# A decode step on one Trainium2 core: set-up reordered around the first tile, norm factors in two parts, a denser cache stream

## The chip, the core and the metric

One core of a Trainium2 chip runs the whole program. The metric is the device time of one execution in microseconds (us). TensorE (PE in the profile) does the matmuls and transposes, VectorE (DVE), ScalarE (ACT) and GpSimd (POOL) the elementwise work; SP issues the plain DMAs and GpSimd the gathers. All arithmetic is fp32: a matmul operand is split into a high and a low part (names ending in hi and lo, or wh and wl), and three products replace one.

## What is computed

One layer step for 512 prompt tokens and 32 sample tokens (8 sequences of 4), whose attention reads a paged cache of 4096 past positions each.

```python
q, k, v, u, gv = split_proj(rms_norm(hp, norm_mix[l]), w_in[l],
                            q_gain[l], k_gain[l], gv_gain[l])
att = prompt_diff_attn(q, k, v, lam)
mix = chunk_gating(u, gv, w_spatial[l], b_spatial[l], GMLP_CHUNK)
hp = hp + merge_out(att, mix, subln_gain[l], lam_init, w_out[l])
hp = hp + sq_relu_ffn(hp, norm_ffn[l], w_up[l], w_down[l])
...
k_past = cache_k[l][page_table].reshape(n_seq_d, n_pages * PAGE_SIZE, N_ATT_HEADS, 2, QK_DIM)
v_past = cache_v[l][page_table].reshape(n_seq_d, n_pages * PAGE_SIZE, N_ATT_HEADS, V_DIM)
att_s = sample_diff_attn(qs, kns, vns, k_past, v_past, lam)
```

`rms_norm` divides by the root mean square and multiplies by a gain; q, k and gv are normalised again per head. `sample_diff_attn` is a softmax over past and new positions, twice per head, and the difference of the two. The model width is 1024, the feed-forward width 4096.

## The kernel before

**Main work.** After `setup`, `in_proj` runs ten pieces of W_in, 256 columns each, in the order q, q, k, k, v, v, gv, gv, u, u. A piece has two halves of the weights' rows and four token tiles of 128; `optB` does a tile and half in 12 matmuls of 128x256 (the block of 12 that the text speaks of). `packed` does the sample tokens' share of a piece in 16 matmuls, from `spk`, the packed sample input. `w_conv` splits a weight half: ScalarE casts wh, VectorE subtracts to get wl. `x_tile` transposes a prompt tile and `split` makes its Thi (ScalarE) and Tlo (VectorE). `post` and `finish_piece` make the norm factors: squares are summed in `ssb`, `rsqrt` raises them to -1/2 on GpSimd (a POOL instruction with `mhalf`), VectorE multiplies (`zn<-zn,ssb`), TensorE transposes (`d<-idt,zn`). Then come the prompt's attention, W_out and eight groups of the feed-forward (`ffn`).

**The stream.** The sample tokens' attention over the cache runs beside this, in 64 chunks of 1 MB of keys and 1 MB of values. `gK` and `gV` gather them (two buffers `kraw`, four `v`), `k_tr` transposes keys on VectorE (kt<-kraw), and issues the gather of chunk n+2 into the buffer it frees; `scores` does two chunks in one block of matmuls (S, the score block, 32 records in the trace), `av` multiplies by values (O), and `fin1`, `fin2` close a sequence: VectorE copies O into `om`, TensorE sums it by a selection matrix (om,selb). `qz_fill` writes a sequence's queries into `qz`. These steps are a list, `micro`; the main work yields a cost after each stretch, and `pump` issues as many steps as the cost pays for, at `TAU` per unit of weight.

**The order.** Each engine runs its instructions in program order. `pinned(True)` keeps the written order; otherwise a scheduler may move instructions of TensorE and VectorE forward, past up to 28 others. Before, `setup` issues the sample input, the page table, the gain in 128 copies (`gm`, 512 KB), weights 0 and 1, prompt tile 0, weights 2 and 3 and the other tiles, and multiplies prompt tiles by `gm` ahead of their transposes (`x_gain`). The sample's queries of both q pieces come ahead of the first piece (`first_q`, `first_keys`), `k_tr` of chunks 0 and 1 with them, and the stream starts there. The third weight half has a buffer of its own, `wq`.

Of the kernel before, what the change touches and what calls it, by code (L numbers as in the profile page):

```python
# [62 lines left out]
def kernel(  # L63
# [88 lines left out]
    wq = big.tile([128, 4 * T], F32R, tag="r3", name="wq")[:, 0:2048].rearrange("p (s k c) -> p s k c", s=2, k=4)  # L152
# [4 lines left out]
    xg = [R[0][:, 1024 * t:1024 * t + 1024] for t in range(2)]  # L157
# [107 lines left out]
    def w_conv():  # L265

        i = st["done"]
        if raws:
            raw = raws.pop(0)
            if i == 3:  # L270
                hi, lo = wq[:, 0], wq[:, 1]
            else:
                pool = pools["w"] if i % 5 > 2 else wp
                hi = pool.tile([128, 4, 256], F32R, tag="wh", name="wh")
                lo = pool.tile([128, 4, 256], F32R, tag="wl", name="wl")
# [119 lines left out]
    def setup():  # L395
        kt0 = kvp.tile([128, 4096], F32, tag="kt", name="kt0")
        xs = kt0[0:32, 0:1024]
        gm = kvp.tile([128, 1024], F32, tag="pp", name="gm")
        fg = kvp.tile([128, 2048], F32, tag="v", name="fg", bufs=VB)
        junk = kvp.tile([128, 512], F32, tag="om", name="junk")  # L400
        ptb = zt_().bitcast(I32).rearrange("p (n q) -> p n q", q=4)
# [11 lines left out]
        for t in range(1, 4):  # L413
            SP.dma_start(out=xt[t], in_=xp[:, t, :])

        G.memset(mhalf, -0.5)
        for t in ssb + [cst]:
            G.memset(t, 1.0)
        kw = dict(base=0, channel_multiplier=0, allow_small_or_imprecise_dtypes=True)
        G.iota(pf[:, 7:8], pattern=[[0, 1]], base=0, channel_multiplier=1, allow_small_or_imprecise_dtypes=True)  # L420
        make_identity(nc, idt)
# [7 lines left out]
        G.memset(gsrc[0:32, :], 0.0)  # L429
# [16 lines left out]
        ps = dt_()  # L446
        for k in range(8):
            PE.transpose(ps[:, 32 * k:32 * k + 32], xsg[:, 128 * k:128 * k + 128], idt[:32, :32])
        keep_warm(5)
        pack(ps[:, 0:256].rearrange("p (k t) -> p k t", k=8), 0, 8)  # L450
        w_conv()
# [4 lines left out]
        x_gain(gm, 0)  # L456
        for n in range(KB):
            gK(n)
        w_conv()
        SP.dma_start(out=gsrc[0:8, :], in_=norm_mix.rearrange("a (k p) -> (a k) p", p=128))  # L460
        SP.dma_start(out=gsrc[8:16, :], in_=norm_ffn.rearrange("a (k p) -> (a k) p", p=128))
        SP.dma_start(out=gsrc[16:20, :], in_=b_spatial.rearrange("a g t -> (a g) t"))
        SP.dma_start(out=gsrc[20:21, 0:64], in_=q_gain)
        SP.dma_start(out=gsrc[20:21, 64:128], in_=q_gain)
        SP.dma_start(out=gsrc[21:22, :], in_=subln_gain)
# [9 lines left out]
        return gm, F, gsrc, junk  # L475
# [16 lines left out]
    def gcols(gsrc):  # L492
        ps = dt_()
        PE.transpose(ps[:, 0:32], gsrc[0:32, 0:128], idt[:32, :32])
        V.tensor_copy(out=gcol, in_=ps[:, 0:32])
# [10 lines left out]
    def params():  # L506
        pinned(True)
# [16 lines left out]
        pinned(False)  # L524
# [58 lines left out]
    def scores(m):  # L583
        b, pj = divmod(m, 4)
        if pj == 0:
            qz_fill(b)
# [113 lines left out]
    TAU = (122.7 + 44.8 * G1 + 30.0 * ATTW) / sum(w for w, _ in micro)  # L700
# [14 lines left out]
    def x_gain(gm, t):  # L715
        (G if t == 3 else V).tensor_tensor(out=xg[t % 2], in0=xt[t], in1=gm, op=ALU.mult)

    def x_tile(t):
        for hf in range(2):
            ps = dt_()  # L720
            for k in range(4):
                kk = 4 * hf + k
                PE.transpose(ps[:, 128 * k:128 * k + 128], xg[t % 2][:, 128 * kk:128 * kk + 128], idt)
            split(ps.rearrange("p (k t) -> p k t", k=4), 4 * hf, t)
# [36 lines left out]
    def finish_piece(kind, p, ss, items):  # L761
# [3 lines left out]
        def stat():  # L765
            rsqrt(ss[:, 0:w * len(items)], EPS if kind in "qk" else 4.0 * EPS)
# [21 lines left out]
        later(stat)  # L788
        for i in range(len(items)):
            later(lambda i=i: norm(i), 1 + i // 2)  # L790
# [45 lines left out]
    def in_proj(gm, F, gsrc, junk):  # L836
        held = []
        pinned(True)
        zq = []

        def first_q(p):
            held.append((w_get(), w_get()))
            sps = dt_()[0:64, 0:256]
            for hf in range(2):
                packed(*held[p][hf], [(4 * hf + b, b) for b in range(4)], sps, hf == 0, hf == 1)
            return sps

        def first_stat(p, sps):
            z = combine(sps)
            zq.append(head_stat(z[0:32], 32, cst[0:32, 4 * p:4 * p + 4], 4))  # L850

        def first_keys():
            x_tile(2)
            k_tr(0)
            for p in range(2):
                q_sample(p, zq[p], cst[0:32, 4 * p:4 * p + 4])
            k_tr(1)
            kv["on"] = True

        sps = first_q(0)  # L860
        x_tile(0)
        w_conv()
        x_gain(gm, 1)
        x_stat(0, [xt[0]], 128, junk, G)
        x_gain(gm, 2)
        x_tile(1)
        x_gain(gm, 3)
        first_stat(0, sps)
        first_stat(1, first_q(1))
        rsqrt(cst[:32, 0:8], EPS)  # L870
        first_keys()
        yield 1.7
        att = attention()
        nt = new_tokens()
        for pi in range(10):
# [10 lines left out]
            if kind == "q":  # L886
                A_, B_ = held[p]
            else:
                A_, B_ = w_get(), w_get()
            for tp in range(2):  # L890
# [5 lines left out]
                for half, w in ((0, A_), (1, B_)):  # L896
                    for t in (2 * tp, 2 * tp + 1):
                        cost = next(att, 0.0) if 2 * pi + tp >= ATT0 else 0.0
                        if half == 0:
                            pss[t] = dt_()[:, 0:256]  # L900
                        optB(pss[t], t, *w, half)
                        if t == 3 and (half == 0 or pi != 1):
# [547 lines left out]
```

## Time and profile before

| | |
|---|---|
| runs | 822.18, 821.0, 822.18 us; median 822.18 |
| profiled execution | 821.3 us, its span 819.6 us |
| mean granted TensorE clock | 0.991 of full speed |
| TensorE busy | 795.7 us (97%) |
| VectorE, ScalarE, GpSimd busy | 537.1 (66%), 358.6 (44%), 178.2 us (22%) |
| DMA | 219 MB, 267 GB/s mean; gathers 134 MB of it |

The span is the time between the first and the last instruction recorded; the execution's own time is 1.7 us more. Busy shares are of the span. All helpers record their operations under line 52 (L52), so operations are told apart by the names of their tiles: `out<-in`.

### The profile page before, as it was taken

The page shows a single profiled execution, that of the slowest core. Times are in us where ns is not written, and L with a number is a line of the kernel's source. Part 1 is how long each engine was busy: PE and PEld are TensorE (multiplying, and loading weights), DVE is VectorE, ACT ScalarE, POOL GpSimd, SP SyncE. Part 2 cuts the span into 40 slices and gives each one's busy share as a digit, 9 for nine tenths or more (in the row PEclk, how much of TensorE's full clock was granted, in tenths as well). Part 3 has the DMA queues.
Part 4 walks back from the last instruction along what each step waited for, and adds up shares of the span by engine and source line. Part 5 has one row for each costly group of instructions (what it writes and reads, how often), then busy time and mean ns, then how long its engine had stood idle before and what let it go on. Part 6 is the DMA issues. An engine that isn't in the chain of part 4 may idle for free.

```text
span 819.6 us, 15373 instructions
## 1 busy us (share of the span) xinstructions
PE 795.7 (97%) x6210; PEld 632.9 (77%) x6210; DVE 537.1 (66%) x883; ACT 358.6 (44%) x892; POOL 178.2 (22%) x196
## 2 busy tenths in 40 slices
PE   5899999999999999999999999998999999999997
PEld 4888887767667888867776777675676999998997
DVE  5878866898997856887677667653464534444254
ACT  4644743776585466463144235234243431331331
POOL 4553431344241222221322321213010000000000
PEclk9799999999999999999999999999999999999999
DMA  8597698787787888877997888877459677576202
GB/s 296 207 391 280 240 344 314 272 317 285 279 321 273 309 310 309 325 283 282 366 366 304 318 325 336 322 264 261 168 182 339 209 244 239 174 239 214 70 18 94
DMA packets 101798, 219.05 MB, mean 267 GB/s; under 512 B 6090, under 2 KB 83999, under 8 KB 85343
## 3 DMA queue, kind: packets, MB, share of 16 engines
q0 software_dynamic: 18432, 134.23, 42.4%
q1 hardware_dynamic: 83294, 83.84, 31.5%
q8 instruction: 49, 0.80, 0.4%
q14 instruction: 23, 0.18, 0.1%
HBM read 213.53 MB, written 4.52 MB: 266 GB/s over the span
## 4 chain that ended last, share of the span: by engine, by line
PE 73%; DVE 8%; issue 8%; ACT 4%; DMA 3%; POOL 2%; SPq 0%; DVEq 0%; POOLq 0%; ACTq 0%
PE d L52 64%; PE S L52 5%; PE O L52 5%; DVE kt L52 2%; ACT PT L52 2%; DMA kraw<-in_cache_k_dram,idxK 2%; DMA v<-in_cache_v_dram,idxK 1%; DMA raw<-in_w_in_dram 1%; ACT wh L52 1%; POOL v L52 1%; DVE zn L52 1%; DVE s L52 1%; POOL ssb L52 1%; DVE wl L52 1%; POOL kraw L52 1%
## 5 line engine op out<-in xcount | busy, mean ns | idle before, releaser
L52 ACT CAST wh<-raw 128x1024 fp32r<-128x1024 f32 x90 | 94.2, 1047 | 175.8 <-PE d L52 139.2
L52 PE MATMUL d<-a,wh 128*128 128x272 f32 (+1 forms) x704 | 168.3, 341 | 0.0
L52 DVE STREAM_TRANSPOSE kt<-kraw 128x2048 f32<-128x2048 f32 x64 | 146.3, 2297 | 16.6 <-PE S L52 7.4
L52 DVE TENSOR_TENSOR wl<-raw,wh 128x1024 fp32r<-128x1024 f32 x90 | 109.7, 1220 | 50.8 <-ACT wh L52 50.4
L52 PEld LDWEIGHTS d<-a,wh 128*128 128x128 f32 x704 | 113.2, 188 | 25.1 <-issue 6.3
L52 PE MATMUL d<-wh,Thi 128*128 128x256 f32 x432 | 127.7, 296 | 1.6 <-ACT t L52 1.6
L52 POOL DMA_INDIRECT v<-in_cache_v_dram,idxK x64 | 64.6, 1009 | 281.3 <-PE O L52 270.9
L52 PE MATMUL d<-wl,Thi 128*128 128x256 f32 x432 | 122.9, 285 | 0.0
L52 PE MATMUL d<-wh,Tlo 128*128 128x256 f32 x432 | 122.3, 284 | 0.0
L52 PE MATMUL d<-Thi,wh 128*128 128x272 f32 (+2 forms) x368 | 108.1, 334 | 0.0
L52 PE MATMUL d<-Tlo,wh 128*128 128x272 f32 (+2 forms) x368 | 106.5, 330 | 0.0
L52 PE MATMUL d<-Thi,wl 128*128 128x272 f32 (+2 forms) x368 | 106.4, 329 | 0.0
L52 PE MATMUL d<-a,wl 128*128 128x272 f32 (+1 forms) x352 | 104.2, 337 | 0.0
L52 PEld LDWEIGHTS d<-wh,Thi 128*128 128x128 f32 x432 | 82.3, 191 | 9.0 <-issue 4.8
L52 POOL DMA_INDIRECT kraw<-in_cache_k_dram,idxK x64 | 69.6, 1088 | 83.8 <-DVE kt L52 49.9
L52 PEld LDWEIGHTS d<-wh,Tlo 128*128 128x128 f32 x432 | 82.3, 191 | 0.4 <-issue 0.4
L52 PEld LDWEIGHTS d<-wl,Thi 128*128 128x128 f32 x432 | 82.1, 190 | 0.4 <-issue 0.4
L52 PEld LDWEIGHTS d<-Thi,wh 128*128 128x128 f32 x368 | 63.5, 188 | 15.6 <-issue 5.4
L52 ACT COPY PT<-d 32x128 f32<-32x128 f32 x256 | 65.6, 256 | 10.7 <-DVE d L52 7.5
L52 PEld LDWEIGHTS d<-Thi,wl 128*128 128x128 f32 x368 | 63.4, 188 | 6.2
L52 PEld LDWEIGHTS d<-Tlo,wh 128*128 128x128 f32 x368 | 63.7, 188 | 5.8
L52 PEld LDWEIGHTS d<-a,wl 128*128 128x128 f32 x352 | 60.5, 188 | 7.4 <-issue 0.4
(270 smaller groups left out, 1063.5 us busy)
## 6 DMA issues: line engine op xcount, KB each, us to landing
raw<-in_w_up_dram SPq DMA_DIRECT2D x32, 512.0 KB, 5.5
raw<-in_w_down_dram SPq DMA_DIRECT2D x32, 512.0 KB, 5.1
plain<-in_w_up_dram SPq DMA_DIRECT2D x20, 512.0 KB, 4.9
plain<-in_w_down_dram SPq DMA_DIRECT2D x20, 512.0 KB, 5.6
raw<-in_w_in_dram SPq DMA_DIRECT2D x18, 512.0 KB, 10.1
raw<-in_w_out_dram SPq DMA_DIRECT2D x8, 512.0 KB, 10.1
plain<-in_w_out_dram SPq DMA_DIRECT2D x8, 512.0 KB, 4.6
r<-in_x_prompt_dram SPq DMA_DIRECT2D x4, 512.0 KB, 9.0
```

The source lines that it names most:

```text
L52: r = f(*args, **kw)
```

## The change

1. `setup`: prompt tile 0, the gain as 8 rows of 128 (`grow`) and weights 0 and 1 are issued first, then the sample input, tile 1, the page table, tiles 2 and 3, weights 2 and 3 (into `w23`, and `wq` goes). `gm` goes: the gain is transposed to a column (`gcol`) and applied to the transposes' result, by ScalarE's scale for tile 0 and a VectorE product for the others (`x_half`).
2. `in_proj`: the first piece goes tile by tile, each tile made one step ahead; the sample input is packed within it, the sample's queries are done inside pieces 0 and 1 like those of other pieces. `k_tr` of chunks 0 and 1 stands in piece 1, and the stream starts at that piece's third tile.
3. `qz_fill` is a step of its own list slot, one ahead of the scores that read it.
4. `early_stat`: the norm factors of a piece's first two tiles (and the sample) are made after half the piece, the others' at its end.
5. `TAU` is smaller.
6. `ffn`, first half of the switch group: a loop issues what is left of the stream but five steps.

```diff
 def setup():
-        SP.dma_start(out=xs, in_=xs_d)
-        SP.dma_start(out=ptb, in_=page_table.rearrange("b l -> (b l)").unsqueeze(0).to_broadcast([128, 256]).rearrange("p (n q) -> p n q", q=4))
-        SP.dma_start(out=gm, in_=norm_mix.to_broadcast([128, 1024]))
+        SP.dma_start(out=xt[0], in_=xp[:, 0, :])
...
+        SP.dma_start(out=grow[0:8, :], in_=norm_mix.rearrange("a (k p) -> (a k) p", p=128))
         w_issue()
         w_issue()
-        SP.dma_start(out=xt[0], in_=xp[:, 0, :])
-        for o in (1024, 3072):
-            w_issue(kt0[:, o:o + 1024].rearrange("p (k c) -> p k c", k=4))
+        SP.dma_start(out=xs, in_=xs_d)
+        SP.dma_start(out=xt[1], in_=xp[:, 1, :])
+        SP.dma_start(out=ptb, in_=page_table...)
+        SP.dma_start(out=xt[2], in_=xp[:, 2, :])
+        SP.dma_start(out=xt[3], in_=xp[:, 3, :])
+        for o in (0, 1024):
+            w_issue(w23[:, o:o + 1024].rearrange("p (k c) -> p k c", k=4))
...
+        keep_warm(6)
+        ps = dt_()
+        PE.transpose(ps[:, 0:32], grow, idt[:32, :32])
+        V.tensor_copy(out=gcol[:, 0:8], in_=ps[:, 0:8])
...
-        keep_warm(8)
-
-        x_stat(4, [xs], 32, junk, G)
-        xsg = kt0[0:32, 2048:3072]
-        V.tensor_tensor(out=xsg, in0=xs, in1=gm[0:32], op=ALU.mult)
+        x_half(0, 0)
         w_conv()
...
+        x_half(0, 1)
+        keep_warm(10)
         w_conv()
+        indices(ptb)
+        return xs, F, gsrc, junk, ptb
...
-    TAU = (122.7 + 44.8 * G1 + 30.0 * ATTW) / sum(w for w, _ in micro)
+    TAU = (100.2 + 44.8 * G1 + 30.0 * ATTW) / sum(w for w, _ in micro)
...
+        if n % 8 == 1 and n < NCH:
+            a.append((qz_fill, (n // 8,)))
...
+    def x_half(t, hf):
+
+        ps = dt_()
+        for k in range(4):
+            kk = 4 * hf + k
+            PE.transpose(ps[:, 128 * k:128 * k + 128], xt[t][:, 128 * kk:128 * kk + 128], idt)
+        xg = R[0][:, 512 * (2 * (t % 2) + hf):512 * (2 * (t % 2) + hf) + 512].rearrange("p (k t) -> p k t", k=4)
+        psv = ps.rearrange("p (k t) -> p k t", k=4)
+        if t == 0:
+            for k in range(4):
+                A.activation(out=xg[:, k], in_=psv[:, k], func=ACTF.Copy, scale=gcol[:, 4 * hf + k:4 * hf + k + 1])
+        else:
+            V.tensor_tensor(out=xg, in0=psv, in1=gcol[:, 4 * hf:4 * hf + 4].unsqueeze(2).to_broadcast([128, 4, 128]),
+                            op=ALU.mult)
+        split(xg, 4 * hf, t)
...
+    def early_stat(kind, ss, items):
+
+        n = (4 if kind in "qk" else 2) * len(items)
+        later(lambda: rsqrt(ss[:, 0:n], EPS if kind in "qk" else 4.0 * EPS))
+        return len(items)
...
+        def first_pass(half, t):
+            if half == 0 and t < 3:
+                x_tile(t + 1)
+            if half == 1:
+                if t < 2:
+                    keep_warm(3)
+                x_stat(t, [xt[t]], 128, junk, G)
+            if t == 0 and half == 1:
+                sample_in(xs)
+                x_stat(4, [xs], 32, junk, G)
...
+                    if pi == 1 and half == 0:
+                        if t < 2:
+                            k_tr(t)
+                        kv["on"] = t >= 2
...
+                if tp == 0 and items:
+                    n0 = early_stat(kind, ss, items)
...
 def ffn(start, joint, last, small, switch=False):
...
                         flush()
                         yield 2.8
+                        if switch and pr == 0 and f == 1:
+                            while kv["i"] < len(micro) - 5:
+                                pump(1.0)
```

How the order moves at the places that matter. First VectorE, from the set-up into the first piece, before (z and zn belong to the sample's queries, kt<-kraw is the first chunk of keys):

```order
L52 TENSOR_REDUCE cst<-z 32x4
L52 TENSOR_TENSOR zn<-d,zn 32x256
L52 TENSOR_SCALAR zn<-zn,cst 32x256
L52 TENSOR_REDUCE cst<-z 32x4
L52 TENSOR_TENSOR Tlo<-d,Thi 128x4x128 x2
L52 STREAM_TRANSPOSE kt<-kraw 128x4x16x32
L52 TENSOR_TENSOR zn<-zn,cst 32x256
```

The same engine in the changed kernel, from the conversion of the third weight half (`w_134` is `w23`, `r_87<-d,gcol` a gain product, `z<-d,gcol` that of the sample input):

```order
L52 TENSOR_TENSOR wl<-w_134,wh 128x1024
L52 TENSOR_TENSOR Tlo<-r_87,Thi 128x4x128
L52 TENSOR_TENSOR r_87<-d,gcol 128x512
L52 TENSOR_TENSOR Tlo<-r_87,Thi 128x4x128
L52 TENSOR_TENSOR z<-d,gcol 128x256
L52 STREAM_TRANSPOSE kt<-kraw 128x4x16x32
L52 TENSOR_TENSOR spk<-z,spk 128x8x32
L52 TENSOR_REDUCE ssb_119<-z 128x4
L52 TENSOR_TENSOR r_87<-d,gcol 128x512
L52 STREAM_TRANSPOSE kt<-kraw 128x4x16x32
L52 TENSOR_TENSOR Tlo<-r_87,Thi 128x4x128
```

The scheduler has moved the two key transposes, written in piece 1, forward to the first piece; the first stands ahead of spk, the second ahead of the third tile's Tlo.

TensorE at the same place in the changed kernel: the second tile's last matmuls of its first half, the transposes of the third tile, and the first packed matmuls.

```order
L52 MATMUL d<-wl,Thi 128x256
L52 MATMUL d<-wh,Tlo 128x256
L52 MATMUL d<-idt,r_89 128x128 x8
L52 MATMUL d<-wh,spk 64x256
L52 MATMUL d<-wl,spk 64x256
```

Before, the packed matmuls of both q pieces stood ahead of every matmul of the first piece; now they follow its third block of 12, and the second half of tile 1 stands behind them.

TensorE at the end of the stream, before (a, wh, wl are the feed-forward's second matmuls):

```order
L52 MATMUL d<-a_4229,wl 128x512
L52 MATMUL O<-v,PT 32x512 x8
L52 MATMUL d<-om,selb_98 64x512
L52 MATMUL d<-lm,selb_98 64x8
L52 MATMUL d<-a_4228,wh 128x512 x2
```

And in the changed kernel, at the last sequence's end:

```order
L52 MATMUL d<-a_4251,wh 128x512 x2
L52 MATMUL d<-a_4251,wl 128x512
L52 MATMUL d<-om,selb_98 64x512
L52 MATMUL d<-lm,selb_98 64x8
L52 MATMUL d<-Thi,wh 128x512
```

Where om,selb stood right behind the O block, eight groups of the feed-forward's matmuls (a with wh twice and wl once) now stand between; so they do at the sequence before.

## Rows read from the trace of the kernel before

**Rows 1.** The page: busy time of the engines.

```profile
PE 795.7 (97%) x6210; PEld 632.9 (77%) x6210; DVE 537.1 (66%) x883; ACT 358.6 (44%) x892; POOL 178.2 (22%) x196
```

**Rows 2.** Stretches: busy us of PE, PEld, DVE, ACT, POOL, then granted clock, DMA share, GB/s.

```profile
0.00:40.00 40.00, 28.45 (x173) 27.02 (x174) 29.07 (x50) 22.41 (x48) 19.25 (x43) 0.84 0.70 249
20.00:25.00 5.00, 4.01 (x19) 4.04 (x20) 4.92 (x11) 1.53 (x3) 4.74 (x7) 0.50 1.05 419
```

**Rows 3.** Timeline of PE, 0 to 61 us: start, duration, operation, idle before and releaser.

```profile
1.92 1.65 PE L52 MATMUL d<-idt,fg 128*128 128x128 f32 x5 [1.92 <-POOL idt masks.py:199]
3.36 3.39 PE L52 MATMUL d<-idt 128*128 128x128 f32 x16
...
15.65 1.07 PE L52 MATMUL d<-idt,r 128*128 128x128 f32 x8 [0.88 <-DVE r L52]
20.99 1.94 PE L52 MATMUL d<-idt,r 128*128 128x128 f32 x8 [4.27 <-DVE r L52]
...
27.29 0.36 PE L52 MATMUL d<-wh,Thi 128*128 128x256 f32 x1
...
30.09 0.29 PE L52 MATMUL d<-wh,Tlo 128*128 128x256 f32 x1
...
41.35 0.85 PE L52 MATMUL S<-kt,qz 128*32 128x256 f32 x12
...
51.84 1.93 PE L52 MATMUL S<-kt,qz 128*32 128x256 f32 x32
...
60.83 0.37 PE L52 MATMUL d<-wh,Thi 128*128 128x256 f32 x1
```

**Rows 4.** Timeline of DVE, 10 to 70 us.

```profile
10.51 1.23 DVE L52 TENSOR_TENSOR wl<-raw,wh 128x1024 fp32r<-128x1024 f32 x1 [1.25 <-ACT wh L52]
11.65 0.42 DVE L52 TENSOR_TENSOR spk<-d,spk 128x256 fp32r<-128x256 f32 x1
...
13.14 1.11 DVE L52 TENSOR_SCALAR idxK<-z,pf 32x64 int32<-32x64 int32 x4
...
22.73 0.69 DVE L52 TENSOR_TENSOR Tlo<-d,Thi 128x512 fp32r<-128x512 f32 x1
...
30.87 2.30 DVE L52 STREAM_TRANSPOSE kt<-kraw 128x2048 f32<-128x2048 f32 x1
...
67.59 2.31 DVE L52 STREAM_TRANSPOSE kt<-kraw 128x2048 f32<-128x2048 f32 x1 [3.35 <-DMA kraw<-in_cache_k_dram,idxK]
```

**Rows 5.** Timeline of POOL, 14 to 54 us.

```profile
14.55 2.04 POOL L52 DMA_INDIRECT kraw<-in_cache_k_dram,idxK  x1 [8.49 <-DVE idxK L52]
...
50.94 2.94 POOL L52 TENSOR_TENSOR ssb<-ssb,mhalf 128x16 f32<-128x16 f32 x1
```

**Rows 6.** ACT: two rows of the timeline, and a group of the page.

```profile
9.43 1.04 ACT L52 CAST wh<-raw 128x1024 fp32r<-128x1024 f32 x1 [4.53 <-DMA raw<-in_w_in_dram]
...
16.32 1.07 ACT L52 CAST Thi<-d 128x512 fp32r<-128x512 f32 x2 [1.55 <-PE d L52]
...
L52 ACT COPY PT<-d 32x128 f32<-32x128 f32 x256 | 65.6, 256 | 10.7 <-DVE d L52 7.5
```

**Rows 7.** Gathers of kraw, issue to landing: the first one; then all 64.

```profile
kraw<-in_cache_k_dram,idxK POOLq DMA_INDIRECT x1, 9.2
...
DMA to landing us min/median/max: 5.6/9.5/12.7
```

**Rows 8.** Timeline of PE at the end of the stream.

```profile
557.43 1.07 PE L52 MATMUL d<-om,selb 128*64 128x512 f32 x2 [2.12 <-DVE om L52]
...
564.25 3.64 PE L52 MATMUL O<-v,PT 128*32 128x512 f32 x32
...
575.47 1.07 PE L52 MATMUL O<-v,PT 128*32 128x512 f32 x8 [0.85 <-DMA v<-in_cache_v_dram,idxK]
```

**Rows 9.** Timeline of PE: the short waits between 60 and 100 us.

```profile
64.00 1.93 PE L52 MATMUL S<-kt,qz 128*32 128x256 f32 x32 [0.51 <-DVE kt L52]
...
97.19 0.44 PE L52 MATMUL d<-idt,zn 128*128 128x128 f32 x2 [0.48 <-ACT r L52]
```

More of the change, by code (lines that the diff above doesn't have):

```diff
@@ L474, in setup, with sample_in @@
         G.tensor_copy(out=idb, in_=idt)
-        return gm, F, gsrc, junk
+    def sample_in(xs):
+        ps = dt_()
+        for k in range(8):
+            PE.transpose(ps[:, 32 * k:32 * k + 32], xs[:, 128 * k:128 * k + 128], idt[:32, :32])
+        xsg = zt_()
+        sv = xsg.rearrange("p (k t) -> p k t", k=8)
+        V.tensor_tensor(out=sv, in0=ps[:, 0:256].rearrange("p (k t) -> p k t", k=8),
+                        in1=gcol[:, 0:8].unsqueeze(2).to_broadcast([128, 8, 32]), op=ALU.mult)
+        pack(sv, 0, 8)
     def masks(F, gsrc):
@@ L712, in pump @@
                 f(*args)
-    def x_gain(gm, t):
-        (G if t == 3 else V).tensor_tensor(out=xg[t % 2], in0=xt[t], in1=gm, op=ALU.mult)
+    def x_half(t, hf):
+        ps = dt_()
+        for k in range(4):
[10 more added lines that the diff above has]
+        split(xg, 4 * hf, t)
     def x_tile(t):
         for hf in range(2):
[L720 to L724, printed above, removed]
+            x_half(t, hf)
     def split(psv, k0, t, col=None):
@@ L786, in tr @@
             tr_pair(z, n, dst, qcol if kind == "q" else None)
-        later(stat)
         for i in range(len(items)):
+            if i == 2:
+                later(stat)
             later(lambda i=i: norm(i), 1 + i // 2)
@@ L834, in post, with in_proj, sample_q, go @@
             SP.dma_start(out=vso[:, cols], in_=vs[:, cols])
-    def in_proj(gm, F, gsrc, junk):
-        held = []
+    def in_proj(xs, F, gsrc, junk, ptb):
         pinned(True)
[L839 to L872, printed above, removed]
+        def first_pass(half, t):
[8 more added lines that the diff above has]
+                x_stat(4, [xs], 32, junk, G)
+            if t == 2 and half == 1:
+                constants()
+            if t == 3 and half == 0:
+                gcols(gsrc)
+        def sample_q(p, z):
+            sc = cst[0:32, 4 * p:4 * p + 4]
+            zs = head_stat(z[0:32], 32, sc, 4)
+            def go():
+                rsqrt(sc, EPS)
+                q_sample(p, zs, sc)
+            later(go)
         att = attention()
@@ new lines, in in_proj @@
+                both = (2 * tp, 2 * tp + 1)
+                steps = [(h, t) for t in both for h in range(2)] if pi == 0 else [(h, t) for h in range(2) for t in both]
+                for half, t in steps:
+                    w = (A_, B_)[half]
+                    cost = next(att, 0.0) if 2 * pi + tp >= ATT0 else 0.0
+                    if half == 0:
+                        pss[t] = dt_()[:, 0:256]
+                    optB(pss[t], t, *w, half)
+                    if t == 3 or (pi == 0 and t == 2 and half == 1):
+                        w_conv()
+                    if t % 2 == 1:
+                        flush()
+                    if pi == 0:
+                        first_pass(half, t)
+                    if half == 1:
+                        post(kind, p, t, pss[t], 128, ss, items)
+                        if pi == 4 and t == 0:
+                            params()
+                        if pi == 4 and t == 3:
+                            params2()
+                        if pi == 9 and t > 0:
+                            cat_tile(t - 1)
+                        if t == 3 and items:
+                            finish_piece(kind, p, ss, items, n0)
+                        if pi == 0 and t == 1:
+                            pinned(False)
+                    elif pi == 5:
+                        next(nt, None)
+                    if pi == 1 and half == 0:
+                        if t < 2:
+                            k_tr(t)
+                        kv["on"] = t >= 2
+                    if pi == 1 and t == 0 and half == 1:
+                        masks(F, gsrc)
+                        load_params()
+                    yield 1.3 + cost
+                    if tp == 0 and t == 1:
```

102 lines of the change are left out of this document (25 added, 77 removed).

## The prediction

> **What bounds the kernel now.** I read the page first. TensorE is busy 97% of the span [rows 1]. So a saving counts only where TensorE stands idle or runs at half clock, or where its own work shrinks; this change leaves its work nearly the same. The idle time is the span less the busy time, 819.6 - 795.7 = 23.9 us. The table of stretches [rows 2] tells where it lies: half of it before 40 us (40 - 28.45 = 11.6), the rest in drops behind it and in the last 20 us. The same rows show a granted clock of 0.50 in 20 to 25 us, that is 1.2 instead of 2.4 GHz, right behind an idle stretch.
>
> The timeline of TensorE over the set-up [rows 3] says what it waits for. It transposes the first prompt tile at 15.65, then stands 4.27 us until VectorE has multiplied the second tile by the gain, and the first matmul of the first piece starts at 27.29. The third piece starts at 60.83, with two score blocks of 1.93 us done by then.
>
> **1. Set-up.** Removed: the 512 KB broadcast of the gain, the gain products ahead of the transposes (one is what TensorE waits for at 20.99), and the sample's query work ahead of the first piece. Added: the tile's transposes first, with the gain applied to their result.
>
> I build the new chain from durations of the trace. The identity is there at 1.92 [rows 3]. Six keep-warm matmuls of 0.21 us, the gain column and the pf transposes take until about 5.0; the first eight transposes (1.07 us [rows 3]) end near 6.8. ScalarE then does four scaled copies of 0.26 us and one Thi cast of 0.54 us (as its copies of 128 columns, and its two casts in 1.07 us) per half, with the 1.04 us weight cast after each [rows 6]: first half at 8.4, first weight at 9.45, second half at 11.05, second weight at 12.1. VectorE's wl follows 1.22 us later [rows 4]: 10.7 and 13.35. So the first matmul of the first piece may start near 10.7 instead of 27.29.
>
> That is not the gain, since the tiles come one at a time, and one thing stands in the way. VectorE writes the gather indices (1.11 us [rows 4]) up to 14.4, as late as now (14.25), so the first gather is issued at 14.45, as now (14.55 [rows 5]). But in the new order the transposition of the first gathered chunk (kt<-kraw, 2.30 us) stands on VectorE right ahead of the product that makes spk, the packed sample input. Before, it stood behind the first piece's tile work and ran at 30.87, when the gather had long landed. VectorE reaches it near 19.4: 14.4 plus three products and casts of 0.69, two more like them, one wl of 1.22 and 0.40, 4.4 us in all, plus some waits. The gather lands at 14.45 + 9.2 = 23.65, as this gather took in the trace [rows 7]. kt then ends at 25.95 and spk, one product of 0.42, at 26.35. TensorE has by then done the first tile, half the second and the third's transposes, and stands ahead of the packed matmuls that read spk, from about 19.2 to 26.4. After an idle stretch of 4 us the clock stayed low for about 5.6 us in the trace (0.50 in 20 to 25 [rows 2]), and I count the same behind this one.
>
> From 26.4 are left of the first piece five blocks of 12 matmuls at 1.43 us (0.12 each: 24 begin from 27.29 to 30.09 [rows 3]), 16 packed matmuls of 0.12, eight transposes and three keep-warm matmuls: 7.2 + 1.9 + 1.1 + 0.6 = 10.8 us, and about 2.5 for the low clock, 39.7. VectorE, with another kt of 2.30 and six Tlo of 0.69 to do behind spk, gives the last tile's Tlo at about 39, and two blocks follow it at 41.1 at most. I take 41.1. The second piece is 8 x 1.43 + 1.9 of packed matmuls + 1.1 of transposes = 14.5: the third starts at 55.6. Before it starts at 60.83 with two score blocks, 60.83 - 3.86 = 56.97 without; after, the stream is turned on later and none is done. Gain 56.97 - 55.6 = **1.4 us**.
>
> Bounds: the landing time is the term, as 9.2 is one of a spread of 5.6 to 12.7 us [rows 7]. At 12.7 kt ends 3.5 later: a loss of 2.1. At 5.6 or less VectorE hardly waits, 4.2 us come back: a gain of 5.6. I take 9.2, the row of the same stretch with the weights moving beside it.
>
> The Trainium skill ("DMA: Bandwidth & Descriptors", section "Anatomy of one DMA — SWDGE (gpsimd) path") has for such a transfer 2.0 us plus the bytes at 436 GB/s, some 4.4 us for one MB as an estimate. By that the chunk is there at 18.9, before VectorE comes to it, and the sum would be that of rival A below. The trace disagrees: 9.2 us here, 5.6 the least.
>
> **2. The end of the stream.** Two stalls stand at its end [rows 8]. At 557.43 the selection matmul (om,selb) waits 2.12 us for VectorE's om, right behind the O block that om is made of. At 575.47 an O block waits 0.85 us for the last v gather. In the new order eight groups of the main matmuls, 5.6 us as from the end of om,selb near 558.6 to the O block at 564.25 [rows 8], stand between the last O block and its om,selb, more than 2.12, and likewise one such stretch at the one before. The O blocks move closer together in front, so a v gather will be late somewhere: 0.6 us, most of 0.85. Sum -2.12 - 0.85 + 0.6 = **-2.4**; ends -3.0 (both gone) and 0 (both come back). The loop that is to put out the stream's rest in the feed-forward stage finds nothing to put out: with and without it the rows of every engine stand alike, so it costs nothing.
>
> **3. Norm factors in two parts.** The power of a whole piece is one GpSimd instruction, 2.94 us for 128x16 [rows 5]; what waits for it is the normalisation, and behind that TensorE's transposes. Its cost to TensorE is bounded by the short waits in the stretch, 0.51 + 0.48 = 1.0 us [rows 9], of which none names the power itself. The two parts cost GpSimd more instructions, between gathers that wait there for a buffer anyway. I take **-0.5**, ends -1.0 and 0.
>
> **4. The denser stream.** TAU makes the stream end at the same place though it starts a piece later. In the new order score blocks stand 0.63, 0.62, 0.5 and 0.5 of a piece apart from piece 2 on, against 0.54 to 0.76 now; a piece is 14.5 us and each block 1.93, so 11.0 and 9.2 us. A score block takes two chunks, one from each of two buffers; a buffer turns around in 9.5 us of landing and 2.3 us of kt, 11.8 us. Two intervals of 9.2 and two of 11.0 fall short by 2 x 2.6 + 2 x 0.8 = 6.8 us if all of it is passed on. Now the like shortfall is nearly all hidden: with blocks 10.5 apart (41.35 and 51.84) the third waited 0.51 [rows 3, 9], though VectorE stood 3.35 for a gather at 67.59 [rows 4]. I take **+1.0**; ends 0 and 6.8. The query tile (qz) one slot sooner moves two VectorE products off the score block's front; no wait of a score block names them in rows 9 (kt is named), so 0.
>
> **The sum.** -1.4 - 2.4 - 0.5 + 1.0 = -3.3. The profiled execution took 821.3 us (span 819.6 and 1.7 around it), the median of the runs is 0.9 above it. 821.3 - 3.3 = **818.0 us**. About 0.2% (1.6 us) is what a measurement of this kernel can tell from no change: faster means under 820.5, slower over 823.8.
>
> **Rivals.**
> A. The first chunk is there when VectorE comes to it (less traffic ahead: the 512 KB broadcast is gone). The rows for: 5.6 us have been seen, against: the DMA share is still 1.05 in 20 to 25 [rows 2], with tiles and weights moving. Set-up -5.6: 821.3 - 5.6 - 2.4 - 0.5 + 1.0 = 813.8. Chance 0.2.
> B. Slower: the gathers can't follow the denser stream. kt waits for its gather in VectorE's program order, and with it all that TensorE needs of VectorE (wl, Tlo). It decides once a turnaround of 11.8 us is more than the interval plus what runs ahead; for it speaks 3.35 us of waiting at 67.59 already now, against it the 0.51 that reached TensorE. With all 6.8, and the first gather 1.4 us later too, which takes the set-up's gain: 821.3 - 2.4 - 0.5 + 6.8 = 825.2. Chance 0.2.
> C. The stream's end doesn't change: the stalls at om and v reappear one block on. For: the end of the stream stands at the same matmul, the loop does nothing; against: the order shows the distance. 821.3 - 1.4 - 0.5 + 1.0 = 820.4. Chance 0.17; the forecast has 0.43.
>
> **How the numbers follow.** The range reaches from below A (813.8, less some of the 1.0 in part 3) most of the way to B: 812.5 to 824.5. Half of C lies within 0.2%, as do small misses of the forecast: faster 0.62, same 0.2, slower 0.18.
>
> **What would show it.** Right: a first matmul of the first piece near 10.7; TensorE idle some 7 us between 19 and 27 with spk or kt as releaser, and VectorE waiting there for kraw; the third piece near 55.6; no wait for om near 557 to 575. Wrong: no such idle stretch (then A), waits of S for kt between 75 and 120 (then B), or the two stalls at the end as before (then C).

## The result and the profile after

The changed kernel takes 839.9 us (median of four runs, 837.21 to 840.91) against 821.97 for the kernel before on the same chip (four runs): a ratio of 1.0218, 95% interval 1.0204 to 1.0232. It is 18 us slower, where 818.0 and a range of 812.5 to 824.5 were forecast. The profiled execution took 837.21 us, its span is 835.5 us and its mean granted clock 0.987; it is the fastest of the four.

The page of the changed kernel, busy time by engine:

```profile
PE 805.3 (96%) x6229; PEld 636.5 (76%) x6229; DVE 535.4 (64%) x887; ACT 360.5 (43%) x900; POOL 183.1 (22%) x218
```

Of the 15.9 us that the span grew, 9.6 are busy time of TensorE (805.3 - 795.7 [rows 1]) though it does the same products, and 6.3 are idle (30.2 against 23.9). By the mean granted clocks, 0.987 and 0.991, lost clock makes some 3.5 us of the 9.6, as an estimate (835.5 x 0.013 less 819.6 x 0.009); what the rest is made of isn't settled here. The stretches say where the idle time and the low clock lie. Columns as in [rows 2]; first the changed kernel:

```profile
0.00:40.00 40.00, 31.29 (x227) 29.20 (x227) 23.70 (x48) 23.22 (x52) 13.41 (x47) 0.96 0.66 218
40.00:60.00 20.00, 15.17 (x122) 14.67 (x122) 10.62 (x23) 8.71 (x19) 13.20 (x14) 0.99 0.51 183
60.00:80.00 20.00, 17.55 (x150) 13.81 (x150) 10.83 (x16) 8.30 (x19) 9.43 (x9) 0.76 0.67 234
100.00:120.00 20.00, 15.42 (x124) 14.08 (x125) 16.05 (x35) 8.91 (x30) 8.08 (x8) 0.83 0.73 253
```

and the same of the kernel before:

```profile
40.00:60.00 20.00, 19.90 (x195) 17.56 (x194) 14.03 (x18) 7.97 (x15) 12.51 (x11) 0.99 1.00 390
60.00:80.00 20.00, 19.42 (x192) 16.69 (x190) 15.34 (x22) 8.13 (x19) 6.45 (x6) 1.00 0.80 292
100.00:120.00 20.00, 20.00 (x193) 17.16 (x192) 14.64 (x35) 10.38 (x31) 8.82 (x7) 1.00 0.92 333
```

The first 40 us are fuller than before (31.29 against 28.45 [rows 2]). The loss stands behind them: TensorE, hardly idle there before, stands 4.8 us between 40 and 60 and 4.6 between 100 and 120, and the clock drops to 0.76 and 0.83. DMA moves 183 GB/s from 40 to 60 where it moved 390: the stream has hardly begun. VectorE is less busy than before from 40 to 80, not more.

The timeline of TensorE in the changed kernel, from the set-up to the fifth piece:

```profile
9.45 0.39 PE L52 MATMUL d<-wh,Thi 128*128 128x256 f32 x1 [0.57 <-ACT wh L52]
...
24.12 0.30 PE L52 MATMUL d<-wh,spk 128*64 128x256 f32 x1 [1.78 <-DVE spk L52]
...
53.67 0.36 PE L52 MATMUL d<-wh,Thi 128*128 128x256 f32 x1
...
58.23 0.39 PE L52 MATMUL d<-wh,Thi 128*128 128x256 f32 x1 [2.89 <-ACT z L52]
...
59.57 0.42 PE L52 MATMUL d<-wl,Thi 128*128 128x256 f32 x1
...
64.99 3.64 PE L52 MATMUL S<-kt,qz 128*32 128x256 f32 x32 [2.34 <-DVE qz L52]
...
99.87 0.39 PE L52 MATMUL d<-wh,Thi 128*128 128x256 f32 x1
...
108.75 0.56 PE L52 MATMUL d<-s,Rm 128*128 128x4 f32 x2 [4.58 <-DVE s L52]
```

The first piece starts at 9.45 instead of 27.29, the third at 53.67 instead of 60.83 [rows 3]. The fifth starts at 99.87; before it starts here, behind the first 4 of 32 matmuls of a score block:

```profile
97.59 0.63 PE L52 MATMUL S<-kt,qz 128*32 128x256 f32 x4
98.20 0.39 PE L52 MATMUL d<-wh,Thi 128*128 128x256 f32 x1
```

So pieces three and four take 46.2 us (99.87 - 53.67) where they took 37.4 (98.20 - 60.83), 8.8 us more. Four score blocks lie in them now, and before only three and those 4 matmuls: that is 1.7 us of the 8.8, and 7.1 remain. Two waits make 2.89 + 2.34 = 5.2, where the waits before came to 1.3 in all (0.51 and 0.48 [rows 9], and one of 0.33). The score block behind the second wait takes 3.64 us where the same block took 1.93 [rows 3], at half clock. The clock fell behind the first wait: from 59.57 on the products begin 0.21 us apart instead of 0.12, ahead of the second wait. Some 7.5 us of matmuls at half clock cost 3.7, and 5.2 - 1.3 + 3.7 = 7.6 is about what is to be explained.

What the two waits stand on is seen one engine further back. VectorE of the changed kernel, then its ScalarE:

```profile
55.13 0.43 DVE L52 TENSOR_TENSOR zn<-zn,ssb 128x256 f32<-128x256 f32 x1 [1.83 <-POOL ssb L52]
...
56.24 0.43 DVE L52 STREAM_TRANSPOSE rows<-zn 32x256 f32<-32x256 f32 x1
...
63.88 0.76 DVE L52 TENSOR_TENSOR zn<-zn,ssb 128x256 f32<-128x256 f32 x2 [2.07 <-POOL ssb L52]
64.56 0.48 DVE L52 TENSOR_TENSOR qz<-qrep,mh 128x128 f32<-128x128 f32 x2
```

```profile
56.71 0.62 ACT L52 COPY qrep<-rows 32x512 f32<-32x512 f32 x1 [3.91 <-DVE rows L52]
57.34 0.47 ACT L52 ACTIVATE zn<-d,cst 128x256 f32<-128x256 f32 x1
57.71 0.47 ACT L52 ACTIVATE z<-d,rst 128x256 f32<-128x256 f32 x1
```

The sample's queries, which stood ahead of the first piece before, are now made inside it and the next. ScalarE stands 3.91 us at the copy qrep<-rows, which waits for VectorE's rows, and these stand in VectorE's order behind a product that waits for norm factors (ssb) from GpSimd. Behind that copy in ScalarE's order is z<-d, which empties the buffer of PSUM, TensorE's output memory, that the matmul at 58.23 needs. At 63.88 VectorE waits for GpSimd's factors again, and the query tiles qz of the first score block stand behind that product.

### The profile page after: what moved, and what is told of

It is laid out like the page before. It is cut to its first block, busy times and chain, and to the rows that moved or that the text cites. A ratio compares the mean times of both kernels' runs of the same rounds, so it can differ in the third digit from the quotient of the medians.

```text
span 835.5 us, 15434 instructions
## 1 busy us (share of the span) xinstructions
PE 805.3 (96%) x6229; PEld 636.5 (76%) x6229; DVE 535.4 (64%) x887; ACT 360.5 (43%) x900; POOL 183.1 (22%) x218
## 4 chain that ended last, share of the span: by engine, by line
PE 66%; issue 9%; DVE 8%; DMA 6%; ACT 5%; POOL 5%; SPq 1%; DVEq 0%; POOLq 0%; ACTq 0%
PE d L52 58%; PE S L52 5%; PE O L52 4%; DVE kt L52 3%; DMA kraw<-in_cache_k_dram,idxK 3%; POOL ssb L52 2%; ACT PT L52 1%; DMA w<-in_w_in_dram 1%; DVE s L52 1%; POOL v L52 1%; DMA v<-in_cache_v_dram,idxK 1%; DMA gg<-in_lambda_q_dram 1%; DVE zn L52 1%; DVE wl L52 1%; POOL cst L52 1%
## 5 line engine op out<-in xcount | busy, mean ns | idle before, releaser
L52 PE MATMUL d<-wh,Thi 128*128 128x256 f32 x448 | 134.2, 300 | 5.8 <-ACT z L52 2.9
L52 PE MATMUL d<-wl,Thi 128*128 128x256 f32 x448 | 128.3, 286 | 2.2 <-DVE wl L52 2.1
L52 PE MATMUL d<-wh,Tlo 128*128 128x256 f32 x448 | 128.2, 286 | 0.8 <-DVE Tlo L52 0.8
L52 PEld LDWEIGHTS d<-wh,Thi 128*128 128x128 f32 x448 | 86.2, 192 | 14.6 <-ACT z L52 4.8
L52 PEld LDWEIGHTS d<-wl,Thi 128*128 128x128 f32 x448 | 86.1, 192 | 2.8 <-DVE wl L52 2.8
L52 PEld LDWEIGHTS d<-wh,Tlo 128*128 128x128 f32 x448 | 86.3, 193 | 1.5 <-DVE Tlo L52 1.5
L52 PE MATMUL S<-kt,qz 128*32 128x256 f32 x1024 | 67.1, 390 | 2.4 <-DVE qz L52 2.3
```

The lines of the kernel that those rows point to most:

```text
L52: r = f(*args, **kw)
```

## The experiments

Every kernel was run 4 to 11 times beside the kernel before on the same chip, whose median lay between 822.5 and 823.4; ratios are to that. For each diff the text says whether it starts from the kernel before or from the change.

**Which part loses?** Theory 1: norm factors in two parts (more instructions on GpSimd, ahead of gathers). Theory 2: the order of the first pieces, with the stream starting late. Theory 3: the smaller TAU, by gathers too dense.

*setup_only*: the change's parts 1 and 2 alone (qz written where it was, no loop at the stream's end, and the few products of `params` held in written order, as before). From the change:

```diff
-    TAU = (100.2 + 44.8 * G1 + 30.0 * ATTW) / sum(w for w, _ in micro)
+    TAU = (122.7 + 44.8 * G1 + 30.0 * ATTW) / sum(w for w, _ in micro)
-                    n0 = early_stat(kind, ss, items)
+                    n0 = 0
...
-            a.append((qz_fill, (n // 8,)))
```

> The kernel before with only the set-up and first piece of the change (parts 1 and 2): one norm factor instruction per piece, qz filled in the scores, TAU as before, no loop, params pinned. Theory 1 (the loss comes from the norm factors in two parts: each early half makes VectorE, in program order, wait for GpSimd): 817 to 823 us, no wait of d<-s,Rm above 1 us near 105. Theory 2 (the loss comes from the first pieces as now written, with the sample's queries and the tiles' norm factors inside them and the stream starting a piece later): 832 to 840. Theory 3 (the loss comes from the smaller TAU, K gathers too dense): 818 to 825.

*rest_only*: the other parts alone, `params` free as in the change. From before:

```diff
+    def early_stat(kind, ss, items):
+        n = (4 if kind in "qk" else 2) * len(items)
+        later(lambda: rsqrt(ss[:, 0:n], EPS if kind in "qk" else 4.0 * EPS))
...
+        if n % 8 == 1 and 1 < n < NCH:
+            a.append((qz_fill, (n // 8,)))
-    TAU = (122.7 + 44.8 * G1 + 30.0 * ATTW) / sum(w for w, _ in micro)
+    TAU = (100.2 + 44.8 * G1 + 30.0 * ATTW) / sum(w for w, _ in micro)
```

> The kernel before with everything but the set-up: norm factors in two parts, qz one slot sooner from the second sequence on, TAU 100.2, the loop, params not pinned; the set-up and first pieces stay. The stream starts as early as before and so ends earlier. Theory 1: 830 to 840 us. Theory 2: 818 to 824. Theory 3: 826 to 838, with waits of VectorE for kraw growing from 5.7 us in all to 15 or more.

*one_stat*: the change with one instruction of norm factors per piece.

```diff
-                    n0 = early_stat(kind, ss, items)
+                    n0 = 0
```

> The changed kernel with one norm factor instruction per piece, as before. Theory 1: 820 to 828 us, the wait of d<-s,Rm at 104 (4.6 us) and that for ACT z at 55 (2.9 us) gone. Theory 2: 835 to 842. Theory 3: 835 to 842.

*tau_back*: the change with only TAU put back to 122.7.

> The changed kernel with TAU 122.7 as before, so that the stream runs less dense and ends later. Theory 1: 834 to 842 us. Theory 2: 834 to 842. Theory 3: 820 to 830.

| kernel | median us | ratio to before [95%] |
|---|---|---|
| setup_only | 855.21 | 1.0382 [1.0364, 1.0400] |
| rest_only | 826.71 | 1.0050 [1.0030, 1.0070] |
| one_stat | 841.12 | 1.0224 [1.0194, 1.0254] |
| tau_back | 854.28 | 1.0367 [1.0334, 1.0400] |

Theory 1 falls: without the two parts the change is as slow (841.1 against 839.9). The loss is in parts 1 and 2. TAU, which theory 3 blames and the prediction charged with a cost, pays 12 to 14 us back (by the ratios, and by the medians): with 122.7 the late stream is still running in the feed-forward groups behind the prompt's. The stretch from 600 to 640 us, first of tau_back, then of the change:

```profile
600.00:640.00 40.00, 29.09 (x136) 16.16 (x138) 19.69 (x39) 12.73 (x20) 5.20 (x5) 0.89 0.46 166
```

```profile
600.00:640.00 40.00, 40.00 (x198) 29.07 (x196) 24.99 (x47) 16.04 (x25) 2.59 (x3) 1.00 0.66 206
```

TensorE is idle for 10.9 us of it in tau_back and for none in the change. It waits there for the stream's last steps, as here in tau_back:

```profile
612.34 1.06 PE L52 MATMUL O<-v,PT 128*32 128x512 f32 x8 [3.12 <-DMA v<-in_cache_v_dram,idxK]
```

**What in parts 1 and 2?** 2a: the stream's later start by itself. 2b: the gathers of chunks 2 and 3, which stand on GpSimd behind the tiles' norm factors. 2c: the crowded first two pieces.

*late_start*: before, with the start of the stream as in the change and its TAU; set-up, queries and norm factors as before.

```diff
-            k_tr(0)
...
-            k_tr(1)
-            kv["on"] = True
...
+                        if pi == 1 and half == 0:
+                            if t < 2:
+                                k_tr(t)
+                            kv["on"] = t >= 2
```

> The kernel before, with the first two key transposes and the start of the stream put off to the second piece as in the change, and TAU 100.2; its set-up, its norm factors and the rest stay as they were. Theory 2a (the loss comes from the stream that starts later and so is behind by two score blocks and runs closer in pieces 2 to 9): 832 to 842 us. Theory 2b (it comes from the gathers of chunks 2 and 3, which in the change stand on GpSimd behind the tiles' norm factors and are issued at 44 and 48 us): 824 to 830. Theory 2c (it comes from the crowded first two pieces, where the sample's queries now stand): 820 to 825.

*early_keys*: the change, with the key transposes written into the first piece.

```diff
+            if t > 1 and half == 0:
+                k_tr(t - 2)
...
-                        if t < 2:
-                            k_tr(t)
```

> The changed kernel with the first two key transposes written into the first piece, behind tiles 2 and 3, so that GpSimd issues the gathers of chunks 2 and 3 ahead of those tiles' norm factors. Theory 2a: 835 to 842 us. Theory 2b: the two gathers issued before 35 us, 822 to 830. Theory 2c: 835 to 842.

*tau_only*: before with TAU at 100.2, nothing else.

> The kernel before with TAU 100.2 alone: the same start of the stream, 5.7% denser, and an earlier end. If the density by itself costs nothing: 818 to 822 us, with no wait for om near the end. If the loss of the run with everything but the set-up (826.7) came from density: 825 to 828. If that came from the norm factors in two parts: 818 to 823.

*fin2_later*: before, a sequence's closing step fin2 half a slot later, to try the prediction's tail by itself.

```diff
-        if m > 0 and m % 8 == 0:
-            (a if m == NCH else c).append((fin2, (m // 8 - 1,)))
+        if m > 1 and m % 8 == 1:
+            a.append((fin2, (m // 8 - 1,)))
```

> The kernel before with the step that sums a sequence by the selection matrix (om,selb) half a list slot later each time, nothing else. If the wait of 2.12 us for om at 557 is a matter of its place behind the O block, that wait is gone and the time is 819 to 821.5; if something else ends late there, no change (821.5 to 824).

| kernel | median us | ratio to before [95%] |
|---|---|---|
| late_start | 834.23 | 1.0146 [1.0110, 1.0183] |
| early_keys | 840.03 | 1.0219 [1.0199, 1.0239] |
| tau_only | 822.78 | 1.0007 [0.9994, 1.0021] |
| fin2_later | 820.02 | 0.9963 [0.9950, 0.9976] |

2a holds for two thirds: the later start, with its TAU, costs 11.7 us (834.23 less 822.54), and tau_only, which differs from late_start in the start alone, is 11.5 faster.

The dense stream alone costs nothing in sum. That is a balance: by the working below tau_only's main work is 8 to 10 us behind between 290 and 550 us, and gets half of it back where its stream ends, with the last O block at 567 us instead of 584. (Its profiled execution, 825.74, is its slowest.) So density isn't cleared as a cause where the stream can't end sooner.

The 3.4 us of rest_only (826.71 less 823.33) lie in the two parts, in qz, in `params` or in the order that the scheduler then chose, which were not told apart; VectorE's waits for gathers grow in it from 5.7 us in all to 12.1, but in tau_only to 10.8 without a loss.

2b finds no support: in early_keys the two gathers are issued at 32.91 and 43.55 instead of 44.23 and 48.28, the second later than was meant, and the time is the change's.

In late_start the waits come behind the start, not at it; its TensorE:

```profile
102.92 0.36 PE L52 MATMUL d<-s,Rm 128*128 128x4 f32 x2 [2.10 <-DVE s L52]
...
110.03 1.93 PE L52 MATMUL S<-kt,qz 128*32 128x256 f32 x32 [2.42 <-DVE mc L52]
...
171.59 0.44 PE L52 MATMUL d<-idt,t 128*128 128x128 f32 x2 [2.47 <-ACT z L52]
```

I set each matmul of the main work beside the same one of the kernel before, and allowed 1.9 us for each S or O block that the one has done by then and the other hasn't. By this working late_start lags 0.6 us at 94 us of the kernel before, 5.5 at 115, 12 at 200 and 15 at 306; the change 4 at the fifth piece's start (98.20), 10 at 107, 13 at 210 and 17 at 306. Both regain 1 to 2 by the end of the span. So the change's waits at 58 and 65 us are its own, and behind 94 and 98 us both lose some 14 us up to 306. One thing that goes along with it is VectorE's waiting for GpSimd's norm factors (zn<-zn,ssb): 6.2 us in all before, 9.6 in the change, 11.6 in late_start, 2.8 in tau_only. No run took that wait away, so it isn't shown to be the cause.

fin2_later is the one version faster than both. Its TensorE at the end of the stream has no wait for om left, against 2.12 us before [rows 8], and a somewhat longer one for v (0.85 before):

```profile
568.42 1.06 PE L52 MATMUL O<-v,PT 128*32 128x512 f32 x8 [1.64 <-DMA v<-in_cache_v_dram,idxK]
```

**Can the set-up's part be had without the late stream?** *gain_after*: before, with the gain as 8 rows and a column applied behind the transposes (`x_half`), and the sample's queries and the stream early as before.

```diff
-        SP.dma_start(out=gm, in_=norm_mix.to_broadcast([128, 1024]))
+        SP.dma_start(out=grow[0:8, :], in_=norm_mix.rearrange("a (k p) -> (a k) p", p=128))
...
-            split(ps.rearrange("p (k t) -> p k t", k=4), 4 * hf, t)
+            x_half(t, hf)
```

> The kernel before with one piece of the change's set-up: the gain as 8 rows, transposed to a column and applied behind the transposes, so that the 512 KB broadcast and the wait for the gain product go; the sample's queries stay ahead of the first piece, the stream starts as early as before, TAU, norm factors and the end of the stream are as before. Theory 2a (the change loses by its late stream, not by this): 816 to 820 us, the 4.27 us wait for r at 21 us gone. Rival (the set-up's new order of work is itself a loss): 823 or more.

*gain_fin2*: the same and fin2_later.

> The run gain_after with fin2_later's edit on top (om,selb half a slot later). If the two gains lie in different places they add: 2.5 us less than gain_after, 813.5 to 818.

*qrep_pool*: the change with the copy qrep<-rows on GpSimd, to take it from ahead of z on ScalarE.

```diff
-                A.copy(out=qrep[32 * q:32 * q + 32].rearrange("p x (h e) m -> p h x e m", h=4),
+                G.tensor_copy(out=qrep[32 * q:32 * q + 32].rearrange("p x (h e) m -> p h x e m", h=4),
```

> The changed kernel with the four copies that replicate the sample's queries (qrep) on GpSimd in place of ScalarE, where they waited 3.9 us for rows and held up what frees PSUM (ACT z) for TensorE at 55 us. If the rest of the loss beside the late stream (about 6 us) is this stall at 55 to 65 us with the low clock behind it: 832 to 837 us, the 2.9 us wait for ACT z gone. If not: 838 to 842.

Measured: gain_after 833.78 us, 1.0132 [1.0115, 1.0149]; gain_fin2 832.56, 1.0113 [1.0096, 1.0130]; qrep_pool 839.73, 1.0225 [1.0194, 1.0257]. In gain_after the rows of the gain, issued on SP behind tiles and weights, come late, and TensorE stands for them:

```profile
11.02 0.31 PE L52 MATMUL d<-idt,z 32*128 32x32 f32 x1 [7.32 <-DMA z<-in_norm_mix_dram]
```

By the working above it is 12.5 us behind at 49 us, so nearly all its loss lies ahead of that. In qrep_pool the wait for ScalarE's z is gone, but the score block waits longer for qz than the two waits were together; its TensorE:

```profile
65.70 3.64 PE L52 MATMUL S<-kt,qz 128*32 128x256 f32 x32 [6.57 <-DVE qz L52]
```

So one wait took the other's place, and the copy's place on ScalarE isn't the cause by itself.

*gain_first*: gain_after with the rows issued second (and their fill with zeros first on GpSimd).

```diff
+        SP.dma_start(out=grow[0:8, :], in_=norm_mix.rearrange("a (k p) -> (a k) p", p=128))
...
-        SP.dma_start(out=gm, in_=norm_mix.to_broadcast([128, 1024]))
```

> The run gain_after with the gain's 8 rows issued second instead of seventh on SP and their fill with zeros first on GpSimd, nothing else. In gain_after TensorE stood 7.3 us for these rows, and all of that run's loss (12 us) was there by 49 us. If the late rows were its cause: 816 to 822 us, no wait for the norm rows above 2 us. If applying the gain behind the transposes is itself slower (VectorE's products stand ahead of Tlo): 825 or more.

*gain_first_fin2*: the same and fin2_later.

> The run gain_first with fin2_later's edit on top. If the two add: 1 to 2.5 us below gain_first; 814 to 820 if that run is at 816 to 822.

*on_later*: the change with the stream on another half piece later, and TAU 96.

```diff
-                        kv["on"] = t >= 2
+                    if pi == 2 and half == 0 and t == 0:
+                        kv["on"] = True
```

> The changed kernel with the stream started at the third piece instead of within the second, and TAU 96 so that it ends at about the same place. If the stalls at 55 to 65 us come from the stream's first step (qz, its copies on ScalarE) being put out before the sample's queries are ready: the 2.3 us wait for qz and the 2.9 us wait for ACT z gone, and 833 to 838 us, though the stream is later still. If the late stream is what costs in all of it: 842 to 850.

Measured: gain_first 828.91 us, 1.0071 [1.0057, 1.0084]; gain_first_fin2 823.94, 1.0022 [1.0012, 1.0032]; on_later 837.97, 1.0197 [1.0178, 1.0216]. fin2_later's edit takes 1.2 us off gain_after and 5.0 off gain_first (2.5 by itself), so such gains don't simply add. gain_first starts the first piece at 23.54, 3.75 us sooner than before, and is yet 6 us behind at 42. Its TensorE and VectorE:

```profile
40.56 0.39 PE L52 MATMUL d<-idt,zn 32*128 32x32 f32 x2 [4.46 <-DVE r L52]
```

```profile
37.52 2.31 DVE L52 STREAM_TRANSPOSE kt<-kraw 128x2048 f32<-128x2048 f32 x1
39.76 0.65 DVE L52 TENSOR_TENSOR r<-d,gcol 128x512 f32<-128x512 f32 x1
```

The gain product now stands between the transposes and everything else, so it is this product that frees TensorE's output buffer; and VectorE comes to it only behind a key transpose of 2.31 us. Before, the gain was multiplied in ahead of the transposes, and TensorE waited for that 0.88 and 4.27 us [rows 3], both ahead of the first piece. In the change itself the set-up came out ahead, so these 6 us aren't shown to be among its 18.

on_later doesn't lose more than the change. Its wait for qz is gone, that for ScalarE's z stays (2.90 us), and one for spk is longer (4.1). The loss doesn't grow with the lateness. But VectorE waits 14.1 us for gathers in it, against 5.9 in the change, and a score block 3.60 us for kt at 94.68: here, with a still smaller TAU, rival B's sign is there.

**Is it that the stream stays behind?** *catch_up*: the change, with the lighter weight that the first 11 slots of the stream have (D0, 0.6 instead of 1) given to eight more, so that it is pushed harder at the start. *catch_up_late*: the same on late_start. The edit of both:

```diff
-        d = D0 if n < LAG else D1 if n >= NCH else 1.0
+        d = D0 if n < LAG + 8 else D1 if n >= NCH else 1.0
```

> The changed kernel with the light weight of the stream's first 11 chunks (0.6) given to the first 19, so that the stream catches up in pieces 2 to 5, where VectorE has slack, and is sparser behind them; its end stays where it was. If the late stream costs because two score blocks with their vector work are pushed into 140 to 260 us, where VectorE was already 89% busy: 830 to 836 us. If the gathers of K can't follow that density: 840 to 850, with VectorE waiting 10 us or more for kraw. If where the blocks stand doesn't matter: 838 to 842.

> The same edit on late_start (834.2). If the place of the blocks is the cost: 825 to 830 us. If not: 832 to 838.

Measured: catch_up 835.86 us, 1.0159 [1.0130, 1.0188], some 0.6% better than the change; catch_up_late 836.71, 1.0152 [1.0126, 1.0178], no different from late_start. So the later start costs by itself, but whether through the place at which blocks then meet the pieces' and the attention's work on VectorE, or through being dense there, stays open.

## Why the prediction was wrong

**The chain of the set-up was right, and its gain about right.** The first matmul came at 9.45 (10.7 forecast), spk at the end of a kt that waits for kraw, as the order showed. But the gather landed sooner. The DMA view of the first gather in the change, against 9.2 us before [rows 7]:

```profile
kraw<-in_cache_k_dram,idxK POOLq DMA_INDIRECT x1, 6.7
```

VectorE waited 0.65 us for it and TensorE 1.78 for spk, not 7.2. The low clock that I had charged behind this wait came ahead of it (0.50 from 19 to 21 us; 0.81 in 20 to 25). The two rows of VectorE:

```profile
21.36 2.31 DVE L52 STREAM_TRANSPOSE kt<-kraw 128x2048 f32<-128x2048 f32 x1 [0.65 <-DMA kraw<-in_cache_k_dram,idxK]
23.59 0.38 DVE L52 TENSOR_TENSOR spk<-z,spk 128x256 fp32r<-128x256 f32 x1
```

The third piece starts at 53.67, against 56.97 without its two score blocks: a gain of 3.3 where 1.4 was forecast, within the ends of -5.6 and +2.1, halfway to rival A. That much was luck. Seven of the versions above have the same set-up (setup_only, one_stat, tau_back, early_keys, qrep_pool, on_later, catch_up). In their profiles and the change's, one each, TensorE waits 1.78 to 6.51 us for spk, and the third piece gains 0.0 to 3.3 us, 1.7 in the middle, so 1.4 was a fair forecast. (The end of -5.6 takes 4.2 us back, where a landing of 5.6 instead of 9.2 gives 3.6.) The Trainium skill ("DMA: Bandwidth & Descriptors", section "Anatomy of one DMA — SWDGE (gpsimd) path") gives some 4.4 us for this transfer as an estimate; 6.7 lies between it and the 9.2 of the trace of before. One landing is a poor guess for the next: this one came at 6.7 and, in tau_back, at 8.6.

**The step that failed is the one that moved the stream's start.** The prediction turned the stream on later, credited the third piece with two score blocks not done, and went on as though these could be done anywhere else at the same price. late_start measures that step, with its TAU: 11.7 us, where part 4 took +1.0. Part 4 looked for a cost in the spacing of the blocks alone, with an end of 6.8; tau_only shows that density costs 0.2 us in sum in the old order, and tau_back that in the new one the smaller TAU pays 12 to 14 back. Rival B named a loss, but by gathers that can't follow. VectorE's waits for gathers are about what they were (5.9 us in all in the change and 4.7 in late_start, 5.7 before), and TensorE's longest rows name s, mc and qz of VectorE. The longest of them, 4.58 us at 108.75 in the change, reads so on VectorE:

```profile
95.63 2.31 DVE L52 STREAM_TRANSPOSE kt<-kraw 128x2048 f32<-128x2048 f32 x1 [2.66 <-DMA kraw<-in_cache_k_dram,idxK]
...
102.51 0.76 DVE L52 TENSOR_TENSOR zn<-zn,ssb 128x256 f32<-128x256 f32 x2 [2.15 <-POOL ssb L52]
...
105.32 0.68 DVE L52 TENSOR_REDUCE s<-S 128x1 f32<-128x512 f32 x1
105.92 2.30 DVE L52 STREAM_TRANSPOSE kt<-kraw 128x2048 f32<-128x2048 f32 x1
108.14 0.12 DVE L52 TENSOR_TENSOR s<-s 128x1 f32<-128x1 f32 x1
```

A gather stands at its head: a key transpose waits 2.66 us for it, and behind that in VectorE's order stand the sums that a piece's norm factors are made of. The piece's normalisation then waits 2.15 us for GpSimd's factors, a sequence's row maxima (s) stand behind it, and between two of their own steps stands a key transpose that waits for nothing. So a late gather takes part, as rival B had it, but it is 2.66 us, and the rest is which instructions of stream and pieces meet in one engine's order.

**A stall that the prediction didn't list.** It removed the sample's queries from ahead of the first piece and counted that as a gain alone. It never asked whose way they stand in inside the pieces. The rows of VectorE and ScalarE above answer it: 7.1 us in pieces three and four, of waits and of half clock. Part 4 put qz at 0 because no score block waited for it; the first one now waits 2.34. This is read from the trace; no run took the queries back out by themselves, and qrep_pool only moved the wait. By this reckoning these 7.1 less the set-up's gain (7.1 - 3.3 = 3.8) are the part of the change's loss that late_start doesn't show: 6 us by the medians, 2.3 by the two profiled spans (835.5 - 833.2).

**Norm factors in two parts:** -0.5 forecast. Taken out of the change they make no difference that the runs can tell (one_stat).

**The end of the stream:** -2.4 forecast, right. The selection matmul has no wait, and an O block waits 1.35 us where 0.6 was taken. TensorE of the change:

```profile
573.90 1.07 PE L52 MATMUL d<-om,selb 128*64 128x512 f32 x2
...
594.34 1.06 PE L52 MATMUL O<-v,PT 128*32 128x512 f32 x8 [1.35 <-DMA v<-in_cache_v_dram,idxK]
```

Over this stretch the change's lag falls by about 2 us, from 18.6, and fin2_later, which has this alone, gains 2.5 (822.54 - 820.02). Rival C falls.

**The range** was built from single prices around one order of the work. Its upper end held 6.8 for gathers and nothing for a stream that starts later, or for query work that moves from a stretch where TensorE was waiting anyway (before 27 us) into one where it was full.

## What to carry to other kernels

Side work in an idle stretch at the start, as the sample's queries here, has cover; put into a full stretch it can stall the engines that share its way. (That is read from the trace; the later start's price is measured.) So when an edit starts side work later, or moves small steps into the main loop, list for each engine what stands behind each moved instruction, above all the copy that empties a buffer the main engine writes next, and price the later start as a term of its own. A short chain moved alone, as fin2 by half a slot, can keep what little the larger change did well.

## What the runs showed of the hardware

Idle time was paid twice. Behind 2.89 us idle at 55 to 58 the products began 0.21 us apart from 59.57 on instead of 0.12, and the score block at 64.99, after 2.34 us more of waiting, took 3.64 us instead of 1.93. The granted clock was 0.76 from 60 to 80 us, with 2.45 us idle in that stretch.

A small transfer issued behind large ones came late here: the 4 KB of the gain, issued at 3.9 us behind tiles and weights, were what TensorE waited for until 11.02 in gain_after; issued second, at 1.26 in gain_first, they held nothing up. The same first gather of one megabyte took 9.2 us before, 6.7 in the change and 8.6 in tau_back, which has the same set-up but for TAU.
